# Second expert layer: 16 prompt tokens leave the dense set and gather their experts' rows instead

## The chip, the cores and the metric

The kernel runs on one core of a Trainium2 chip. The metric is the device time of one execution in microseconds (us), as the median of several runs. The engines are TensorE (PE, with its weight loads as PEld), VectorE (DVE), ScalarE (ACT), GpSimd (POOL) and SyncE (SP, which issues most DMAs).

## The reference, cut to what matters

The kernel is one inference step of a trunk with two layers over 304 tokens (T): 16 meta tokens, 256 prompt tokens and 32 sample tokens. Each layer is a mixer followed by an expert layer, and only the expert layer is touched here. It picks, per head, the 16 best of 128 x 128 single-neuron experts:

```python
s1 = einsum('thd,hkd->thk', q[..., :128], keys[:, 0])     # 8 heads, 128 keys
s2 = einsum('thd,hkd->thk', q[..., 128:], keys[:, 1])
v1, i1 = top_k(s1, 16); v2, i2 = top_k(s2, 16)
sc, pos = top_k(v1[..., :, None] + v2[..., None, :], 16)  # best 16 of 256
eidx = i1 * 128 + i2 at pos                               # one of 16384 experts
gate = softmax(sc)
act  = gelu(einsum('thkd,td->thk', u_tab[eidx], x))
y    = einsum('thk,thkd->td', gate * act, v_tab[eidx])    # rows of 1024
```

u_tab and v_tab hold 16384 rows of 1024 floats, 64 MB each.

## The kernel before, in words

`peer(l)` is the expert layer, called for layer 0 and layer 1. It treats most tokens as dense: for 256 of them every expert is evaluated, and a matrix G of gate values (zero where an expert isn't chosen) weighs the results. The other `ng` tokens are gathered: their chosen rows are fetched one by one. In layer 0, 48 tokens are gathered, as two groups of 16 and 32 tokens; in layer 1, whose meta tokens need no expert output (`d0` = 16), it is one group of 32.

Dense part. The 16384 experts are 128 blocks of 128. For a block `e`, `up_load` loads 128 rows of u (512 KB, tile `raw`), `up` multiplies them with the dense tokens into one PSUM tile `ps_u`, and a Gelu on ACT stores `act`. The first 24 blocks (nf) use full fp32 operands, of which each matmul shows as two records; the other 104 split each operand in a high and a low part (`wh` by ACT, `wl` by DVE) and take three matmuls for each of the 8 slices of the model dimension, 24 in all. `weigh` (L1029) multiplies `act` by G and splits it again (`ch`, `cl`, tiles `sc` and `qs`); `down` takes two token tiles of 128 by 512 output columns by three products, 12 matmuls, added up in `ps_mm` through all blocks. The last four blocks are kept for the end, where they are multiplied transposed ("ends"). 42 `act` tiles exist, so that 36 blocks of `up` (ahead) run before the first `down`.

G. `ggroup` builds G for 8 tokens at a time with four DVE operations, 16 matmuls in f16 and two copies by ACT, and writes 16 tokens at a time to DRAM. `gates_load` (L1013) reads it back for 8 blocks at once (1 MB, tile `gb`); the tag `gb` has four buffers, used also for the staging of G and for `xr2` and `yac` of the gathered tokens.

Gathered part. `gprep` spreads the gathered tokens' expert numbers, gates and rows over 128 partitions (8 lanes for 16 tokens, 4 for 32). For each group, `rows` fetches rows of u by an indirect DMA on POOL (128 rows, 512 KB, tile `ab`), `gup` on DVE multiplies and adds up, `gact` is the Gelu; then the same for v with `gdown`, and `gsum` adds the lanes up on TensorE.

What sets the order. Every step has a due time in `at(due, step)`; steps are emitted in that order, and the language's scheduler then places the instructions of each engine by its own estimates, so that one may pass another. Each engine runs its list strictly in that order: an instruction that waits holds up all those behind it. `late` ties the gathered steps to the last marked DVE operation. The due times hang on `tg` (start of `ggroup`), `tw` (first `down`, after all `ggroup`s), and `te` (end).

Of the kernel before, what the change touches and what calls it, by code (L numbers as in the profile page):

```python
# [8 lines left out]
F32 = mybir.dt.float32  # L9
# [30 lines left out]
def _consts():  # L40
    c = {}
    eye = np.eye(P, dtype=np.float32)
    one = np.ones((P, P), np.float32)
    c["k_all"] = np.concatenate(
        [eye, one / 1024, one / 256, np.tile(np.arange(P, dtype=np.float32), (P, 1))], axis=1)
    sm = np.ones((P, T), np.float32)
    for o, _ in CHUNKS:
        sm[:, o] = 0
    gid = np.zeros(T, np.int64)
    for i, (o, n) in enumerate(CHUNKS):  # L50
        gid[o:o + n] = i
    att = np.zeros((P, 3, P), np.float32)
    for i, (o, n) in enumerate(TT):
        for s in range(n):
            for t in range(s, n):
                att[s, i, t] = gid[o + s] == gid[o + t]
    km = np.zeros((P, 11), np.float32)
    km[:, 0] = (np.arange(P) // 16) % 2 == 0
    km[:, 1] = (np.arange(P) // 16) % 2 == 1
    km[:16, 2] = 1  # L60
    for s in range(8):
        km[16 + 4 * s:20 + 4 * s, 3 + s] = 1
    c["k_diag"] = np.concatenate(
        [np.arange(P)[:, None] % n == np.arange(n)[None] for n in (32, 16)], axis=1).astype(np.float32)
    p, r = np.arange(P)[None], np.arange(P)[:, None]
    c["k_rep"] = np.stack([r == 16 + p % 32, (r == p % 16), (r == p % 32), r // 32 == p // 32, r // 16 == p // 16],
                          axis=1).astype(np.float32)
    hs = np.eye(4, dtype=np.float32)
    xm = ((r // 32 == np.arange(64)[None] // 16) & (r % 32 < 16)).astype(np.float32)
    c["k_gla"] = np.concatenate([sm, att.reshape(P, -1), km, np.tile(hs.reshape(1, 16) / 128, (P, 1)), xm], axis=1)  # L70
    c["k_hsel"] = np.ascontiguousarray(np.repeat(hs[:, :, None], P, 2))
    rs = np.ones((P, T), np.float32)
    rs[:, 0:TP:64] = 0
    rs[:, TP::4] = 0
    q = np.arange(P)
    bo = (q[:, None] // 64 == q[None] // 64).astype(np.float32)
    r = np.arange(64)
    grp = np.where(r < 16, 0, np.where(r < 48, 1 + (r - 16) // 4, 9))
    ma = np.zeros((2, P, 2, 64), np.float32)
    for j in range(2):  # L80
        same = np.ones((64, 64), bool) if j == 0 else (grp[:, None] == grp[None]) & (grp[:, None] < 9)
        for o in range(2):
            ma[j, 64 * o:64 * o + 64, 0] = same & (r[:, None] < r[None])
            ma[j, 64 * o:64 * o + 64, 1] = same & (r[:, None] <= r[None])
    lv = np.stack([((q[:, None] // (2 * m) == q[None] // (2 * m)) & ((q[:, None] // m) % 2 == 1)
                    & ((q[None] // m) % 2 == 0)) | (q[:, None] == q[None]) for m in (1, 2, 4, 8, 16, 32)], axis=1)
    cm = np.tile(grp[None] == 0, (P, 1))
    rm = np.tile((grp[:, None] == np.arange(9)[None]), (2, 1))
    c["k_rwkv"] = np.concatenate(
        [rs, bo / 64, bo, cm, rm, bo[:, ::64] / 64], axis=1).astype(np.float32)  # L90
    c["k_inv"] = np.concatenate(
        [ma[0].reshape(P, P), ma[1].reshape(P, P), lv[:, 0].T, lv[:, 1:5].reshape(P, 4 * P)], axis=1).astype(np.float32)
    return c
# [88 lines left out]
class Prog:  # L182
# [564 lines left out]
    def peer(self, xh, xl, l):  # L747
# [1 line left out]

        nc, a = self.nc, self.a  # L750
        d0 = 0 if l == 0 else NM
        g0 = d0 + 256
        ng = T - g0
        tiles = [(d0, P), (d0 + P, P), (g0, ng)]
        groups = ([(0, 16)] if ng == 48 else []) + [(ng - 32, 32)]
        with ExitStack() as es:
            pp = es.enter_context(self.tc.tile_pool(name=f"pe{l}", bufs=1, reuse_waits="tile"))
            self.psum_banks(mm=4, u=2, s=2)
# [2 lines left out]
            pr = es.enter_context(self.tc.tile_pool(name=f"pr{l}", bufs=1, side="right", reuse_waits="tile"))  # L761
            ab = lambda shape, dt=F32: self.t(pr, shape, dt, "ab", 3)
            gb = lambda shape, dt=F32: self.t(pr, shape, dt, "gb", 4)
            G = self.t(dp, [16, P, P, 16], F32, "G")
            self.extra(pp, 3, 1)
            es.callback(self.extra, None, 0, 0)
            units = []
# [15 lines left out]


            keys = gb([P, 16, P])
            kr = tl([P, 5, P], "k_rep")
            krep, kblk = kr[:, :3, :], kr[:, 3:, :]

            vals2 = tl([P, 16, 2, 16], "vals"), tl([P, 8, 2, 16], "valsg")
            idx2 = tl([P, 16, 2, 16], "idx", 1, U32), tl([P, 8, 2, 16], "idxg", 1, U32)  # L790
# [7 lines left out]
            def whole32():  # L798
                x32.extend(tl([P, 4, 256], n) for n in ("wh", "wl"))
                self.turn.update(wh=-1, wl=-1)  # L800
                for k in range(KB):
                    nc.vector.tensor_tensor(x32[k // 4][:, k % 4, :], f(xh[:, k, d0:d0 + 256]),
                                            f(xl[:, k, d0:d0 + 256]), op=ALU.add)

            qst, pq0 = {}, []

# [183 lines left out]

            def up(e):
                wh, wl = wts.pop(("u", e))
                pu = self.psum("u")[:, :256]
                if wl is None:
                    for k in range(KB):
                        mm(nc, pu, wh[:, k, :], x32[k // 4][:, k % 4, :], k == 0, k == KB - 1)
                else:
                    mm3(nc, pu, lambda k: wh[:, k, :], lambda k: wl[:, k, :],
                        lambda k: xh[:, k, d0:d0 + 256], lambda k: xl[:, k, d0:d0 + 256])
                acts[e] = tl([P, 256], "act", NR)  # L1000
                nc.scalar.activation(acts[e], pu, AF.Gelu_apprx_tanh)  # L1001

            Y, ends = [], []
# [5 lines left out]
                                         None, hl if hl is None else (hl[:, 0], hl[:, 1]))  # L1009

            def gates_load(e):
                gr.append(gb([P, 16, 8, 16]))
                nc.sync.dma_start(gr[-1].rearrange("p b i t -> p b (i t)"),  # L1013
                                  G[:, :, e:e + 8, :].rearrange("b p i t -> p b (i t)"))

            def weigh(e):

                if e % 8 == 0:
                    gr[0] = gr.pop(1)
                if e >= P - NL:  # L1020
                    ch, cl = (tl([P, 256], "act", NR, F32R) for _ in range(2))
                elif e % 2:
                    cc = tl([P, 2, 256], "qs", 3, F32R)
                    ch, cl = cc[:, 0, :], cc[:, 1, :]
                else:
                    ch, cl = (tl([P, 256], "sc", 6, F32R) for _ in range(2))
                c = acts.pop(e)
                v16 = lambda ap: ap.rearrange("p (b t) -> p b t", t=16)
                self.mark[True] = nc.vector.tensor_tensor(v16(c), v16(c), gr[0][:, :, e % 8, :], op=ALU.mult)  # L1029
                split(nc, c, ch, cl)  # L1030
                coef[e] = ch, cl

            def down(e):
# [8 lines left out]
                for i in range(2):  # L1042
                    for j, (c, v) in enumerate(((ch, vh), (ch, vl), (cl, vh))):
                        for q in range(2):
                            mm(nc, Y[2 * q + i], c[:, i * P:(i + 1) * P],
                               v[:, 4 * q:4 * q + 4, :].rearrange("p k d -> p (k d)"),
                               e == 0 and j == 0, e == P - NL - 1 and j == 2)

# [9 lines left out]
            def gprep():  # L1058
# [11 lines left out]
                for g, (r0, n) in enumerate(groups):  # L1070
                    er, gt, eg = tl([P, n], f"er{g}", 1, I32), tl([P, n], f"gt{g}"), tl([P, n], "gres", 2)
                    o = 0 if n == 32 else 1
                    rep = krep[:ng, 2 * l + o, :]
                    for src, dst in ((ei, eg), (gates[2], gt)):
                        pt = self.psum("s")
                        mm(nc, pt[:, :P], rep, src[:ng])
# [77 lines left out]
            tg = ps + pp_["pl"]  # L1154
            for i in range(2):
                at(tg + 0.1 * i, turn, i)
            for q in range(32):
                at(tg + 1 + pp_["gs"] * q, ggroup, q)
            tw = tg + 1 + 32 * pp_["gs"] + pp_["gl"]

            for j, step in enumerate(pairs(1)):
                at(tg + 1.1 + pp_["gs"] * (8 + 1.5 * j), step)
            at(tg + 1.1 + pp_["gs"] * 31, gprep)
            ahead, u0, u1 = pp_["ahead"], pp_["u0"], pp_["us1"]
            n0 = int((tg - u0) / u1)
            for e in range(P):
# [15 lines left out]
            t1 = tw + pp_["g2"]  # L1182
            te = tw + 2 * tu * (P - ahead) + tu * ahead
            tg = (te - pp_["te"] - 15 - t1) / (2 * len(gc))
            for j, (g, c) in enumerate(gc):
                for s, fn, tab in ((0, gup, "u"), (len(gc), gdown, "v")):
                    late(t1 + tg * (j + s), rows, tab, g, c)
                    for r in range(2):
                        late(t1 + tg * (j + s + pp_["gj"] * r) + self.lag, fn, g, c, r)
            for g in range(len(groups)):  # L1190
                late(t1 + tg * len(gc) + self.lag - 0.5, gact, g)
            late(te - pp_["te"], gsum)
            for q in range(2):
                late(te - pp_["te"], xsum, q)
# [19 lines left out]
            for k in range(KB):  # L1214
                if k % 2 == 0:
                    YT[k // 2] = self.psum("u" if k < 4 else "mm")
                o = YT[k // 2][:, (k % 2) * 256:(k % 2) * 256 + 256]
                for j, args in enumerate(ends):
                    into(o, k, *args, j == 0 and k % 2 == 0, False)
                for i in range(2):  # L1220
                    mm(nc, o[:, i * P:(i + 1) * P], Ys[:, 2 * (k // 4) + i, (k % 4) * P:(k % 4 + 1) * P], self.ident,
                       False, i == 1)
                xk = X[k // 4][:, k % 4, :]
                nc.vector.scalar_tensor_tensor(z(k)[:, d0:g0], xk[:, d0:g0], ALPHA, o, op0=ALU.mult, op1=ALU.add)
# [585 lines left out]
```

## Time and profile before

| | us |
|---|---|
| median of 3 runs | 2565.35 (2559.76 to 2567.32) |
| the profiled execution, its own time | 2568.89 |
| its span, first to last instruction | 2567.1 |
| PE busy in it | 2420.2 (94%) |
| layer 1: first fp32 `up` | 1707.6 |
| layer 1: G built | 1778 to 1896 |
| layer 1: first `down` | 1918.17 |
| layer 1: last `down` | 2528 |

A time in the rows below is the start in us from the span's first instruction; matmuls overlap, so the time that one takes on PE is read from the distance between two starts, not from its duration.

### The profile page before, as it was taken

The numbers are of one execution on the slowest core, as the hardware profiler recorded it, in microseconds if no ns is written. First come the engines' busy times: TensorE is split into PE (matmuls) and PEld (weight loads), VectorE is DVE, ScalarE is ACT, GpSimd is POOL, SyncE is SP. The second block draws the span as 40 slices with busy tenths as digits, with TensorE's granted clock in tenths as the row PEclk, the third lists the DMA queues.
The fourth block names the chain that finished last, engine by engine and source line by source line (L and its number), as shares of the span: only waits on it lengthen the run. The fifth ranks groups of instructions, "written<-read, shape, count | busy, mean of one in ns | idle before, by whom it ended". The sixth has DMA issues, their size and how long they took to land.

```text
span 2567.1 us, 41284 instructions
## 1 busy us (share of the span) xinstructions
PE 2420.2 (94%) x15394; PEld 2073.1 (81%) x15402; DVE 1854.4 (72%) x4200; ACT 1155.6 (45%) x2054; POOL 550.5 (21%) x620
## 2 busy tenths in 40 slices
PE   7989989899999999988999988899989999999997
PEld 5878879799998898865666656787979999989986
DVE  5555898777767888766777785679767766677775
ACT  7524335444444445523544443432444444444453
POOL 3435100011111222024334233520010101121200
PEclk9978999999999999989999999899999999999998
DMA  5323246897879978622111102323679767797662
GB/s 160 114 73 124 99 153 229 283 308 284 285 272 304 364 274 286 240 94 85 48 50 46 40 29 91 119 89 140 233 261 314 245 245 254 261 338 263 242 220 72
DMA packets 197873, 489.73 MB, mean 191 GB/s; under 512 B 21396, under 2 KB 91428, under 8 KB 192936
## 3 DMA queue, kind: packets, MB, share of 16 engines
q1 hardware_dynamic: 173480, 401.10, 44.6%
q0 software_dynamic: 23040, 83.90, 9.7%
q8 instruction: 121, 1.98, 0.3%
q10 hardware_dynamic: 1152, 2.10, 0.2%
q14 instruction: 80, 0.66, 0.1%
HBM read 447.41 MB, written 39.63 MB: 190 GB/s over the span
## 4 chain that ended last, share of the span: by engine, by line
PE 75%; DVE 13%; issue 3%; DMA 3%; ACT 3%; POOL 2%; SPq 1%; POOLq 0%; ACTq 0%; DVEq 0%
PE ps_mm L162 33%; PE ps_u L162 24%; PE ps_s L162 7%; PE ps_pj L162 4%; PE ps_iv L162 3%; DMA gb<-G 3%; PE ps_ch L162 1%; DVE wl L171 1%; PE ps_po L162 1%; DVE ab L921 1%; ACT wh L170 0%; DVE ab L923 0%; DVE x L1575 0%; DVE x L375 0%; DVE ab L918 0%
## 5 line engine op out<-in xcount | busy, mean ns | idle before, releaser
L170 ACT ACTIVATE wh<-raw 128x1024 fp32r<-128x1024 f32 x529 | 560.3, 1060 | 634.4 <-PE ps_u L162 302.1
L171 DVE TENSOR_TENSOR wl<-raw,wh 128x1024 fp32r<-128x1024 f32 x481 | 594.2, 1236 | 301.9 <-ACT wh L170 295.9
L162 PE MATMUL ps_u<-xh,wl 128*128 128x256 f32 x1664 | 469.8, 282 | 5.5 <-DVE wl L171 5.5
L162 PE MATMUL ps_u<-xh,wh 128*128 128x256 f32 x1664 | 471.8, 284 | 2.6 <-ACT act L1001 2.6
L162 PE MATMUL ps_u<-xl,wh 128*128 128x256 f32 x1664 | 468.2, 281 | 0.0
L162 PEld LDWEIGHTS ps_u<-xh,wh 128*128 128x128 f32 x1664 | 314.7, 189 | 11.4 <-ACT act L1001 3.0
L162 PEld LDWEIGHTS ps_u<-xl,wh 128*128 128x128 f32 x1664 | 314.4, 189 | 8.9 <-issue 0.8
L162 PEld LDWEIGHTS ps_u<-xh,wl 128*128 128x128 f32 x1664 | 314.3, 189 | 6.9 <-DVE wl L171 6.6
L162 PE MATMUL ps_mm<-wh,sc 128*128 128x512 f32 x992 | 292.0, 396 | 12.3 <-ACT sc L170 12.3
L162 PE MATMUL ps_mm<-wh,qs 128*128 128x512 f32 x992 | 291.8, 396 | 0.0
L1092 POOL DMA_INDIRECT ab<-in_u,er x80 | 76.8, 961 | 862.9 <-DVE ab L1099 478.7
L162 PEld LDWEIGHTS ps_mm<-wh,sc 128*128 128x128 f32 x992 | 181.8, 190 | 46.6 <-ACT sc L170 12.7
L162 PEld LDWEIGHTS ps_mm<-wh,qs 128*128 128x128 f32 x992 | 181.5, 189 | 35.0
L1092 POOL DMA_INDIRECT ab<-in_v,er x80 | 103.8, 1298 | 431.6 <-DVE gb L1113 339.2
L162 PE MATMUL ps_mm<-wl,sc 128*128 128x512 f32 x496 | 155.4, 395 | 0.1
L162 PE MATMUL ps_mm<-wl,qs 128*128 128x512 f32 x496 | 155.2, 394 | 0.0
L1001 ACT ACTIVATE act<-ps_u 128x256 f32<-128x256 f32 x256 | 94.1, 368 | 105.8 <-PE ps_u L162 105.8
L162 PE MATMUL ps_mm<-xh,wh 128*128 128x304 f32 x416 | 134.0, 326 | 8.1 <-ACT xh L353 4.2
L162 PE MATMUL ps_s<-ab 128*128 128x128 f16 x1024 | 133.6, 296 | 1.7 <-ACT gb L970 1.3
L162 PE MATMUL ps_mm<-xh,wl 128*128 128x304 f32 x416 | 130.1, 313 | 3.9 <-POOL wl L171 3.3
L171 POOL TENSOR_TENSOR wl<-raw,wh 128x1024 fp32r<-128x1024 f32 x48 | 115.2, 2405 | 79.9 <-ACT wh L170 72.5
L162 PE MATMUL ps_mm<-xl,wh 128*128 128x304 f32 x416 | 130.4, 314 | 1.8 <-POOL xl L358 1.8
(559 smaller groups left out, 4492.2 us busy)
## 6 DMA issues: line engine op xcount, KB each, us to landing
raw<-in_ut SPq DMA_DIRECT2D x256, 512.0 KB
raw<-in_v SPq DMA_DIRECT2D x256, 512.0 KB
G<-gb SPq DMA_DIRECT2D x32, 1024.0 KB
gb<-G SPq DMA_DIRECT2D x32, 1024.0 KB
raw<-in_wq SPq DMA_DIRECT2D x32, 512.0 KB
raw<-in_w_in SPq DMA_DIRECT2D x20, 512.0 KB
raw<-in_w_out SPq DMA_DIRECT2D x8, 512.0 KB
raw<-in_w_k SPq DMA_DIRECT2D x8, 512.0 KB
```

The lines of the kernel that those rows point to most:

```text
L162: nc.tensor.matmul(out, lhsT, rhs, start=start, stop=stop, skip_group_check=True)
L170: nc.scalar.activation(h, src, AF.Copy)
L171: return (eng or nc.vector).tensor_tensor(l, src, f(h), op=ALU.subtract)
L921: nc.vector.tensor_tensor(eqj, eqj, ib[:n, :, None, :].to_broadcast([n, 16, 16, nh]), op=ALU.mult)
L1001: nc.scalar.activation(acts[e], pu, AF.Gelu_apprx_tanh)
L1092: nc.gpsimd.indirect_dma_start(out=w[:, j, :], out_offset=None, in_=a[f"{tab}{l}"], in_offset=bass.IndirectOffsetOnAxis(ap=gst[g][0][:, c ...
```

## The change

Layer 1 takes 240 dense tokens instead of 256 (`ND = (256, 240)`). The 16 prompt tokens that leave join the 32 sample tokens: 48 are gathered, in the two groups that layer 0 has. The dense tokens still make two tiles of 128, which now start at 0 and at 112 and overlap by 16 tokens. `up`, its Gelu, the weighing and the splits run over 240 columns; `down` keeps its matmuls as they are (the 16 tokens of the overlap are computed twice, and one of the two is left out at the end). G has 15 pieces instead of 16, so 30 `ggroup` steps instead of 32, and every due time behind them moves up by two such steps, 5.7 units. There are 32 more gathers of 128 rows, 16 for u and 16 for v, with 16 more `gup` and 16 more `gdown`. The delay `lag` between a gather and its use is now a minimum of three terms: 20 becomes 19.29 in both layers.

```diff
+ND = (256,240)
...
-        g0 = d0 + 256
+        nd = ND[l]
+        g0 = d0 + nd
         ng = T - g0
-        tiles = [(d0, P), (d0 + P, P), (g0, ng)]
-        groups = ([(0, 16)] if ng == 48 else []) + [(ng - 32, 32)]
+        toff = (0, nd - P)
+        tiles = [(d0 + o, P) for o in toff] + [(g0, ng)]
+        groups = [(0, ng - 32)] * (ng > 32) + [(ng - 32, 32)]
...
-                c = slice(i * P, (i + 1) * P)
+                c = slice(toff[i], toff[i] + P)
...
-                pu = self.psum("u")[:, :256]
+                pu = self.psum("u")[:, :nd]
...
-                            mm(nc, Y[2 * q + i], c[:, i * P:(i + 1) * P],
+                            mm(nc, Y[2 * q + i], c[:, toff[i]:toff[i] + P],
...
-            for q in range(32):
+            for q in range(nd // 8):
                 at(tg + 1 + pp_["gs"] * q, ggroup, q)
-            tw = tg + 1 + 32 * pp_["gs"] + pp_["gl"]
+            tw = tg + 1 + (nd // 8) * pp_["gs"] + pp_["gl"]
...
-            at(tg + 1.1 + pp_["gs"] * 31, gprep)
+            at(tg + 1.1 + pp_["gs"] * max(nd // 8 - 1, 27.75), gprep)
...
+            lag = min(self.lag, 2.4 * tg, 14 + tg / 2)
...
-                        late(t1 + tg * (j + s + pp_["gj"] * r) + self.lag, fn, g, c, r)
+                        late(t1 + tg * (j + s + pp_["gj"] * r) + lag, fn, g, c, r)
...
-                    mm(nc, o[:, i * P:(i + 1) * P], Ys[:, 2 * (k // 4) + i, (k % 4) * P:(k % 4 + 1) * P], self.ident,
+                    mm(nc, o[:, i * P:nd if i else P], Ys[:, 2 * (k // 4) + i, (k % 4) * P:(k % 4 + 1) * P], self.ident[:, i * (2 * P - nd):],
```

Beyond these counts the scheduler's lists come out differently at three places of layer 1; layer 0's lists move by a few DVE rows.

SP, at the first loads of gates (`gb<-G`) behind the last pieces of G. Before:

```order
501 L972 DMA G_15998<-gb_18671 128x2048
502 L249 DMA raw_18979<-in_ut 128x1024
503 L249 DMA raw_19017<-in_v 128x1024
504 L1013 DMA gb_18901<-G_15998 128x16x128
505 L249 DMA raw_19035<-in_ut 128x1024
506 L249 DMA raw_19075<-in_v 128x1024
507 L249 DMA raw_19093<-in_ut 128x1024
508 L1013 DMA gb_19260<-G_15998 128x16x128
509 L249 DMA raw_19131<-in_v 128x1024
```

The same place of the changed kernel:

```order
499 L252 DMA raw_18930<-in_v 128x1024
500 L252 DMA raw_18948<-in_ut 128x1024
501 L979 DMA G_15998<-gb_18619 128x2048
502 L1020 DMA gb_18870<-G_15998 128x15x128
503 L1020 DMA gb_19214<-G_15998 128x15x128
504 L1020 DMA gb_19698<-G_15998 128x15x128
505 L1020 DMA gb_20163<-G_15998 128x15x128
506 L252 DMA raw_18986<-in_v 128x1024
507 L1020 DMA gb_20629<-G_15998 128x15x128
508 L1020 DMA gb_21092<-G_15998 128x15x128
509 L1020 DMA gb_21558<-G_15998 128x15x128
510 L252 DMA raw_19004<-in_ut 128x1024
```

Two or three loads of weights stood between two loads of gates; now seven loads of gates have one load of weights among them, and the next weights (`raw_19004`) stand behind all seven.

DVE, from the first weighing (L1029, L1036 in the changed kernel) on; `wl` is the low part of a block of weights, which an `up` or a `down` needs. Before:

```order
2586 L1029 TENSOR_TENSOR act_16949<-act_16949,gb_18901 128x256
2587 L1029 TENSOR_TENSOR act_16984<-act_16984,gb_18901 128x256
2588 L1029 TENSOR_TENSOR act_17047<-act_17047,gb_18901 128x256
2589 L171 TENSOR_TENSOR sc_18904<-act_16949,sc_18903 128x256
2590 L1029 TENSOR_TENSOR act_17080<-act_17080,gb_18901 128x256
2591 L1029 TENSOR_TENSOR act_17259<-act_17259,gb_18901 128x256
2592 L171 TENSOR_TENSOR wl_19020<-raw_19017,wh_19019 128x1024
2593 L171 TENSOR_TENSOR qs_18957<-act_16984,qs_18957 128x256
```

In the changed kernel the first weighing is row 2579. Rows 2579 to 2618 are 33 weighings (the last of them reads the fifth load, `gb_20629`), six splits of weighed tiles and one `wl`; then:

```order
2614 L1036 TENSOR_TENSOR act_18341<-act_18341,gb_20163 128x240
2615 L1036 TENSOR_TENSOR act_18426<-act_18426,gb_20163 128x240
2616 L1036 TENSOR_TENSOR act_18514<-act_18514,gb_20163 128x240
2617 L1036 TENSOR_TENSOR act_18608<-act_18608,gb_20163 128x240
2618 L1036 TENSOR_TENSOR act_18763<-act_18763,gb_20629 128x240
2619 L174 TENSOR_TENSOR wl_18840<-raw_18837,wh_18839 128x1024
2620 L1036 TENSOR_TENSOR act_18796<-act_18796,gb_20629 128x240
2621 L174 TENSOR_TENSOR wl_18896<-raw_18893,wh_18895 128x1024
```

`wl_18840` belongs to the `up` that PE has in its list right before the first `down` (`ps_u_18843`). Before, two to eight weighings stood between two `wl`.

ACT, at the first splits of weighed tiles (`sc` and `qs`). Before, the Gelus (`act<-ps_u`, L1001) of the last blocks of `up` stood ahead of the first of them:

```order
1507 L1001 ACTIVATE act_18827<-ps_u_18802 128x256
1508 L170 ACTIVATE wh_18926<-raw_18924 128x1024
1509 L1001 ACTIVATE act_18860<-ps_u_18835 128x256
1510 L170 ACTIVATE wh_18981<-raw_18979 128x1024
1511 L1001 ACTIVATE act_18899<-ps_u_18874 128x256
1512 L170 ACTIVATE sc_18903<-act_16949 128x256
```

The same place of the changed kernel, where L1008 is the Gelu:

```order
1502 L173 ACTIVATE sc_18872<-act_16949 128x240
1503 L173 ACTIVATE qs_18926<-act_16984 128x240
1504 L173 ACTIVATE sc_18981<-act_17047 128x240
1505 L173 ACTIVATE qs_19040<-act_17080 128x240
1506 L173 ACTIVATE sc_19095<-act_17259 128x240
1507 L173 ACTIVATE qs_19154<-act_17272 128x240
1508 L173 ACTIVATE wh_18833<-raw_18831 128x1024
1509 L1008 ACTIVATE act_18763<-ps_u_18738 128x240
1510 L173 ACTIVATE wh_18839<-raw_18837 128x1024
```

Six splits, which need weighed tiles, now stand ahead of the Gelu of `ps_u_18738`. `ps_u` has two banks, so the second `up` after that one has to wait for this Gelu. PE's own list has 96 matmuls of `up` between the last matmul of G and the first `down` before; now it has 46 up to that wait, 24 behind it (`ps_u_18804`), and 24 more (`ps_u_18843`) that need `wl_18840`.

DVE, at the second run of weighings, behind `gact` (`ha<-ha,gt`), where the buffers of `xr2` come free. In the changed kernel four loads of gates are weighed here (32 weighings) in rows 2871 to 2902; between them stand `wl_22189` (row 2878) and `wl_22207` (row 2885), and then:

```order
2899 L1036 TENSOR_TENSOR act_21938<-act_21938,gb_23890 128x240
2900 L1036 TENSOR_TENSOR act_21997<-act_21997,gb_23890 128x240
2901 L1036 TENSOR_TENSOR act_22056<-act_22056,gb_23890 128x240
2902 L1036 TENSOR_TENSOR act_22115<-act_22115,gb_23890 128x240
2903 L174 TENSOR_TENSOR wl_22246<-raw_22243,wh_22245 128x1024
```

Before, the first 32 of these weighings have nine `wl` among them (rows 2860 to 2906).

## Rows read from the trace of the kernel before

**Rows 1.** The page: busy time of each engine, share of the span, instructions.

```profile
PE 2420.2 (94%) x15394; PEld 2073.1 (81%) x15402; DVE 1854.4 (72%) x4200; ACT 1155.6 (45%) x2054; POOL 550.5 (21%) x620
```

**Rows 2.** Busy time by stretches, clock as a share of 2.4 GHz.

```profile
core 0: us, PE busy (x) PEld busy (x) DVE busy (x) ACT busy (x) POOL busy (x), PEclk, DMA share, GB/s
600.00:664.00 64.00, 64.00 (x415) 58.36 (x414) 49.04 (x66) 30.92 (x47) 9.36 (x10) 1.00 0.79 284
1749.00:1753.00 4.00, 4.00 (x11) 3.23 (x12) 4.00 (x23) 0.17 (x1) 0.00 (x0) 0.57 0.02 4
1778.00:1896.00 118.00, 115.85 (x858) 108.78 (x857) 100.48 (x180) 56.31 (x95) 0.00 (x0) 0.99 0.59 217
1918.00:1922.00 4.00, 3.83 (x9) 3.06 (x10) 4.00 (x11) 2.56 (x7) 0.00 (x0) 0.50 1.12 339
2048.00:2112.00 64.00, 64.00 (x408) 57.95 (x407) 42.40 (x54) 31.21 (x48) 7.50 (x8) 1.00 0.72 253
```

**Rows 3.** Timeline of PE, one `up` of layer 1: start, duration, instruction.

```profile
2049.95 0.28 PE L162 MATMUL ps_u<-xh,wh 128*128 128x256 f32 x1
...
2052.80 0.63 PE L162 MATMUL ps_mm<-wh,sc 128*128 128x512 f32 x2
```

**Rows 4.** Timeline of PE, matmuls of other widths.

```profile
180.41 0.30 PE L162 MATMUL ps_mm<-yl,wh 128*128 128x304 f32 x1
180.55 0.30 PE L162 MATMUL ps_mm<-yh,wl 128*128 128x304 f32 x1
...
1710.43 1.89 PE L162 MATMUL ps_u<-wl,raw 128*128 128x256 f32 x8
...
1781.37 2.04 PE L162 MATMUL ps_s<-ab 128*128 128x128 f16 x16
...
2534.20 0.60 PE L162 MATMUL ps_u<-k_all,ab 128*128 128x128 f32 x4
2534.64 0.39 PE L162 MATMUL ps_mm<-k_all,ab 128*128 128x128 f32 x2
```

**Rows 5.** The lines of `gsum` on PE: durations, first and last start.

```profile
L162 PE MATMUL ps_s<-k_diag,gb x16: 193/276/276, 2512.2 to 2513.8; 128*128 128x32 f32 x16
```

**Rows 6.** Timeline of PE around the first `down`, idle time in brackets.

```profile
1748.95 1.55 PE L162 MATMUL ps_u<-wh,raw 128*128 128x256 f32 x4 [4.52 <-ACT act L1001]
...
1895.72 0.77 PE L162 MATMUL ps_s<-ab 128*128 128x128 f16 x5
...
1899.48 1.88 PE L162 MATMUL ps_s<-ab,k_rep 32*128 32x512 f32 x4
...
1911.49 0.28 PE L162 MATMUL ps_u<-xl,wh 128*128 128x256 f32 x1
1918.17 1.22 PE L162 MATMUL ps_mm<-wh,sc 128*128 128x512 f32 x2 [6.40 <-ACT sc L170]
```

**Rows 7.** Timeline of SP's queue, from the first load of gates on.

```profile
1902.03 0.38 SPq L1013 DMA_DIRECT2D gb<-G  x1
...
1934.78 0.43 SPq L1013 DMA_DIRECT2D gb<-G  x1
...
2232.80 0.43 SPq L1013 DMA_DIRECT2D gb<-G  x1
```

**Rows 8.** Timeline of DVE: weighings (L1029) and splits.

```profile
1917.24 1.10 DVE L1029 TENSOR_TENSOR act<-act,gb 128x256 f32<-128x256 f32 x3 [5.27 <-DMA gb<-G]
1918.25 0.42 DVE L171 TENSOR_TENSOR sc<-act,sc 128x256 fp32r<-128x256 f32 x1
...
1943.40 0.76 DVE L1029 TENSOR_TENSOR act<-act,gb 128x256 f32<-128x256 f32 x2 [0.67 <-DMA gb<-G]
...
2240.18 0.76 DVE L1029 TENSOR_TENSOR act<-act,gb 128x256 f32<-128x256 f32 x2 [2.16 <-DMA gb<-G]
```

**Rows 9.** Timeline of PE: its idle time at the second run of weighings.

```profile
2277.30 0.39 PE L162 MATMUL ps_u<-xh,wl 128*128 128x256 f32 x1 [1.41 <-DVE wl L171]
```

**Rows 10.** DVE by lines, 1896 to 2530: busy, mean ns, idle before.

```profile
L171 DVE TENSOR_TENSOR wl<-raw,wh 128x1024 fp32r<-128x1024 f32 x220 | 270.2, 1229 | 156.6 <-ACT wh L170 155.5
```

More of the change, by code (lines that the diff above doesn't have):

```diff
@@ L65, in _consts @@
     p, r = np.arange(P)[None], np.arange(P)[:, None]
-    c["k_rep"] = np.stack([r == 16 + p % 32, (r == p % 16), (r == p % 32), r // 32 == p // 32, r // 16 == p // 16],
+    c["k_rep"] = np.stack([r == 16 + p % 32, (r == p % 16), (r == p % 32), r == 32 + p % 32,
+                             r // 32 == p // 32, r // 16 == p // 16],
                           axis=1).astype(np.float32)
@@ L751, in peer @@
         d0 = 0 if l == 0 else NM
-        g0 = d0 + 256
+        nd = ND[l]
+        g0 = d0 + nd
         ng = T - g0
-        tiles = [(d0, P), (d0 + P, P), (g0, ng)]
-        groups = ([(0, 16)] if ng == 48 else []) + [(ng - 32, 32)]
+        toff = (0, nd - P)
+        tiles = [(d0 + o, P) for o in toff] + [(g0, ng)]
+        groups = [(0, ng - 32)] * (ng > 32) + [(ng - 32, 32)]
+        reps = {(0, 16): 1, (0, 32): 2, (16, 32): 0, (32, 32): 3}
         with ExitStack() as es:
@@ L763, in peer @@
             gb = lambda shape, dt=F32: self.t(pr, shape, dt, "gb", 4)
-            G = self.t(dp, [16, P, P, 16], F32, "G")
+            G = self.t(dp, [nd // 16, P, P, 16], F32, "G")
             self.extra(pp, 3, 1)
@@ L785, in peer @@
             keys = gb([P, 16, P])
-            kr = tl([P, 5, P], "k_rep")
-            krep, kblk = kr[:, :3, :], kr[:, 3:, :]
+            kr = tl([P, 6, P], "k_rep")
+            krep, kblk = kr[:, :4, :], kr[:, 4:, :]
             vals2 = tl([P, 16, 2, 16], "vals"), tl([P, 8, 2, 16], "valsg")
@@ L801, in whole32 @@
                 for k in range(KB):
-                    nc.vector.tensor_tensor(x32[k // 4][:, k % 4, :], f(xh[:, k, d0:d0 + 256]),
-                                            f(xl[:, k, d0:d0 + 256]), op=ALU.add)
+                    nc.vector.tensor_tensor(x32[k // 4][:, k % 4, :nd], f(xh[:, k, d0:d0 + nd]),
+                                            f(xl[:, k, d0:d0 + nd]), op=ALU.add)
             qst, pq0 = {}, []
@@ L992, in up @@
                 wh, wl = wts.pop(("u", e))
-                pu = self.psum("u")[:, :256]
+                pu = self.psum("u")[:, :nd]
                 if wl is None:
                     for k in range(KB):
-                        mm(nc, pu, wh[:, k, :], x32[k // 4][:, k % 4, :], k == 0, k == KB - 1)
+                        mm(nc, pu, wh[:, k, :], x32[k // 4][:, k % 4, :nd], k == 0, k == KB - 1)
                 else:
                     mm3(nc, pu, lambda k: wh[:, k, :], lambda k: wl[:, k, :],
-                        lambda k: xh[:, k, d0:d0 + 256], lambda k: xl[:, k, d0:d0 + 256])
-                acts[e] = tl([P, 256], "act", NR)
+                        lambda k: xh[:, k, d0:d0 + nd], lambda k: xl[:, k, d0:d0 + nd])
+                acts[e] = tl([P, 256], "act", NR)[:, :nd]
                 nc.scalar.activation(acts[e], pu, AF.Gelu_apprx_tanh)
@@ L1011, in gates_load @@
             def gates_load(e):
-                gr.append(gb([P, 16, 8, 16]))
+                gr.append(gb([P, 16, 8, 16])[:, :nd // 16])
                 nc.sync.dma_start(gr[-1].rearrange("p b i t -> p b (i t)"),
@@ L1020, in weigh @@
                 if e >= P - NL:
-                    ch, cl = (tl([P, 256], "act", NR, F32R) for _ in range(2))
+                    ch, cl = (tl([P, 256], "act", NR, F32R)[:, :nd] for _ in range(2))
                 elif e % 2:
                     cc = tl([P, 2, 256], "qs", 3, F32R)
-                    ch, cl = cc[:, 0, :], cc[:, 1, :]
+                    ch, cl = cc[:, 0, :nd], cc[:, 1, :nd]
                 else:
-                    ch, cl = (tl([P, 256], "sc", 6, F32R) for _ in range(2))
+                    ch, cl = (tl([P, 256], "sc", 6, F32R)[:, :nd] for _ in range(2))
                 c = acts.pop(e)
@@ L1072, in gprep @@
                     o = 0 if n == 32 else 1
-                    rep = krep[:ng, 2 * l + o, :]
+                    rep = krep[:ng, reps[r0, n], :]
                     for src, dst in ((ei, eg), (gates[2], gt)):
@@ L1188, in peer @@
                     for r in range(2):
-                        late(t1 + tg * (j + s + pp_["gj"] * r) + self.lag, fn, g, c, r)
+                        late(t1 + tg * (j + s + pp_["gj"] * r) + lag, fn, g, c, r)
             for g in range(len(groups)):
-                late(t1 + tg * len(gc) + self.lag - 0.5, gact, g)
+                late(t1 + tg * len(gc) + lag - 0.5, gact, g)
             late(te - pp_["te"], gsum)
@@ L1216, in peer @@
                     YT[k // 2] = self.psum("u" if k < 4 else "mm")
-                o = YT[k // 2][:, (k % 2) * 256:(k % 2) * 256 + 256]
+                o = YT[k // 2][:, (k % 2) * 256:(k % 2) * 256 + nd]
                 for j, args in enumerate(ends):
```

## The prediction

> **What bounds the kernel now.** I read the page first: PE is busy 94% of the span, DVE 72%, and the other engines less [rows 1]. An average says little, so the stretches come next. Deep in layer 1's expert stage PE is busy for all 64.00 us of a 64 us stretch, at full clock (2.4 GHz), with DVE at 42.40 us and the DMA engines at 0.72 [rows 2]. There every nanosecond of a matmul counts, and nothing else does. Then I looked for the places where PE isn't full: while G is built (115.85 of 118 us, with DVE at 100.48 [rows 2]); right before the first `down`, where PE is idle for 6.40 us until a weighed tile comes [rows 6]; and one wait of 1.41 us for a `wl` in the second run of weighings [rows 9]. The first of these two has a cause that the rows show: DVE waits for the first load of gates, issued at 1902.03 and weighed from 1917.24 on, 15.2 us later [rows 7, 8], while PE has run out of `up` work at 1911.6 [rows 6]. So two things decide: how much shorter the matmuls get, and whether PE goes on being fed at those places.
>
> **What gets shorter.** The profiled execution took 2568.89 us, 3.5 more than the median; I make the sum as a difference and apply it to the median, 2565.35.
>
> *Split `up`.* 24 matmuls take from 2049.95 to 2052.80 [rows 3], 118.8 ns each at 256 columns. At 304 columns the distance is 140 ns [rows 4], so a column costs about 0.44 ns and 240 columns would take 111.8 ns, unless a floor comes first. What the floor is the trace doesn't show at this shape. The nearest rows have 128 columns: 110 ns from 2534.20 to 2534.64 (four), and 118 ns in the f16 products of G (16 in 2.04 us, less about 0.27 for the last one's own length) [rows 4]. Gain per matmul between 0.8 and 7.0; I take 6.5, since the row at 110 ns has the same unstrided weights and the f16 row reads its weights with a stride. 104 blocks x 24 = 2496 matmuls: **-16** (0 to -17.5). The Trainium skill (TensorE: Matmul & The Clock Gate, section on LDWEIGHTS) says that a weight load costs by its columns, about columns / 1.2 ns; for 128 that is an estimate of 107 ns, which speaks against any gain below some 107 ns; the row at 110 agrees, the f16 row at 118 does not, and by the first the gain stays near -16, by the second it falls to -2.
>
> *fp32 `up`.* Eight records end 1.89 us after the first starts; with 0.3 to 0.4 for the last one's own length they start 213 to 227 ns apart [rows 4], I take 216; at 240 of 256 columns that is 202. 24 blocks x 16 records x 13.5 ns: **-5** (0 to -5.5).
>
> *G.* Two `ggroup` steps fewer are 32 matmuls of 118 ns: **-4**. But G's stretch has DVE at 85% and PE idle for only 2.15 us [rows 2]; the `up`s in it shrink by some 3 us while DVE's work per step stays, so PE waits for DVE instead. I give back **+3.5** (0 to +7).
>
> *Ends.* 96 matmuls of 256 columns: **-0.5**. Sum of the gains: -25.5, and -22 after G.
>
> **What is added.** `gprep`'s second group costs PE some 2.3 us (1.88 for four records of 512 columns [rows 6], and the small ones); it falls into the wait before the first `down` and is counted there. `gsum`'s second group is 16 more records: 16 from 2512.2 to 2513.8, 0.107 each [rows 5]: **+1.7**, with nothing beside it. 32 more gathers, 16 `gup` and 16 `gdown` go to POOL, the DMA queues and DVE. Layer 0 gathers 48 tokens already: there, PE is busy 64.00 of 64 us with DVE at 49.04 and DMA at 0.79 [rows 2]. So in steady state they are hidden: 0 (to +6, if layer 1 gets less room).
>
> **What the new order costs.** Two places, both on the chain to the end since PE makes up for nothing later.
>
> *First `down`.* Before, PE has 96 `up` matmuls after G's last one and works until 1911.6, 15.4 us [rows 6]. Now it reaches the wait for a PSUM bank after 46: 15.4 - 96 x 0.119 + 46 x 0.112 + 2.3 = 11.5 us. That bank is freed by a Gelu which ACT has behind six splits of weighed tiles. The first weighing came 21.0 us after G's last matmul (1896.2 to 1917.24 [rows 6, 8]); six weighings and five splits at 0.335 (three from 1917.24 to 1918.25 [rows 8]) are 3.7, and a weight split on ACT, priced like DVE's 1.23 [rows 10], makes it about 4.9 more until the Gelu. If the gates land as late as before, PE waits 21.0 + 4.9 - 11.5 = 14.4 us; if 4 us sooner, since no weight loads are queued ahead of the second load, 10.4. I take 12.4. Then come 24 matmuls (2.7 us), and the next `up` needs `wl_18840`, behind 33 weighings of which the last needs the fifth load of gates. Three `gb` buffers are free at that point, so the fourth load waits for the first eight weighings (about 5 us after the first) and the fifth for the next eight (about 9). From issue to first weighing a load takes 8.6 us (1934.78 to 1943.40) or 7.4 (2232.80 to 2240.18) [rows 7, 8]: the fifth can be weighed 17 us after the first, and `wl` takes 1.23 [rows 10]. PE is through with its 24 matmuls about 7.6 us after the first weighing, so it waits 18.4 - 7.6 = 10.8 us more. Together 23 against 6.4: **+16.8**. Ends: +4 (if the loads land in a row and DVE is through its 33 weighings in 11 us) and +26 (if only two buffers are free).
>
> *Second run of weighings.* Between `wl_22144`, the last one ahead of `gact`, and `wl_22246` DVE has 32 weighings, fed by four loads, and only two `wl`. The fourth load can start once the first has been weighed: 7.4 for the first, 4.1 for its eight weighings and a `wl`, 8.5 for the fourth, 3 for its weighings and the `wl`: 23 us. PE uses a `wl` each 2.8 us (24 `up` in 2.85 [rows 3]), so three of them last 8.4 us, and DVE is at most two ahead (5.6): PE waits between 9 and 14.6 us; I take 11.9, against 1.4 now [rows 9]: **+10.5** (0, if the loads come early enough, to +13).
>
> *Clock.* After the idle time of 6.40 us PE's clock is at 0.50 (1.2 GHz) for a whole stretch of 4 us, and after one of 4.52 at 0.57 [rows 6, 2]. Each such stretch of 4 us costs about half of its length. One exists now; the new waits make three or four: **+4** (0 to +8).
>
> Sum: -25.5 + 3.5 + 1.7 + 16.8 + 10.5 + 4 = **+11**. Forecast: 2565.35 + 11 = 2576 us (2580 in a profiled execution); with every term within half of its bounds, 2564 to 2590.
>
> **The rivals.**
> *PE stays fed* (faster). The lists only look bad: seven loads of gates run back to back and land early, weighings at 0.335 us go past quickly, and the weights behind them arrive in time. The waits then stay near those of before, and -22 + 1.7 plus about 2 for each place gives -16: 2549. For it: steady stretches have DVE at 66% [rows 2], room to catch up. Against it: the `wl` that PE needs stands behind a fifth load that can't start before DVE has weighed sixteen blocks. It decides if the two places together cost less than about 12 us. Chance 0.17.
> *The up matmuls keep their 119 ns* (slower still). If the floor is that of the f16 row, 14 of the -16 are lost: 2590. For it: a weight load goes with each matmul, and 128 columns of f16 take 118 [rows 4]. Against it: 110 in the other row. Chance 0.13.
> *The loads take longer.* Six gathers, three loads of gates and two of weights now start together while the DMA engines already show 1.12 of their share [rows 2]; at 15 us per load in place of 8, the first `down` costs another 14 and the second run 7: 2597. Chance 0.1.
> *In between* (no change): only one of the two places waits, -16 + 13 = -3 or so: 2563. Chance 0.12.
> That leaves 0.48 for the forecast.
>
> **How the numbers follow.** Within 0.3% is 7.7 us, about what a measurement of this kernel can tell from no change. Faster by more: the first rival, 0.17. Slower by more: both slower rivals, and of the forecast the part above 2573, some 0.42: 0.65. The rest is 0.18. The range reaches to the rival that is faster, and on the other side to 2603, so that each end leaves out about one in ten.
>
> **What would show it.** Right: start distances of 111 to 113 ns in layer 1's `up`; idle time of PE of some 12 us ended by ACT and some 10 ended by DVE `wl` before the first `down`; several waits for `wl` in the second run, 10 to 14 us in all; clock 0.5 after each. Wrong: distances near 119; waits before the first `down` under 10 us together; or PE idle in the steady stretch with POOL's gathers or the DMA share near 1, which would mean that the added gathers aren't hidden.

## The result, and the profile after

The changed kernel takes 2586.31 us (median of 11 runs) against 2567.32 before (11 runs): ratio 1.0077, 95% interval 1.0054 to 1.0099, some 19 us slower. Forecast was 2576 in a range of 2549 to 2603, slower by 11. Its profiled span is 2587.0 us, against 2567.1 before; the two spans differ by 1.2 us where layer 1's expert stage starts, so the rest is all in that stage.

The page, busy time of each engine (answers to [rows 1]):

```profile
PE 2422.8 (94%) x15394; PEld 2075.3 (80%) x15394; DVE 1879.9 (73%) x4246; ACT 1151.7 (45%) x2053; POOL 621.1 (24%) x652
```

PE's busy time hardly moved, which hides both sides: shorter matmuls, and others drawn out by a halved clock (PEclk 0.50 in the rows below). The stretches show more (columns as in [rows 2]):

```profile
1775.00:1889.00 114.00, 107.83 (x809) 102.92 (x808) 100.41 (x210) 54.14 (x90) 0.00 (x0) 0.96 0.60 213
1903.00:1915.00 12.00, 0.29 (x3) 0.10 (x2) 4.73 (x15) 3.42 (x9) 0.00 (x0) 0.67 1.14 325
1915.00:1920.00 5.00, 5.00 (x24) 5.00 (x25) 5.00 (x14) 1.07 (x2) 0.00 (x0) 0.50 0.87 234
1920.00:1927.00 7.00, 0.82 (x4) 0.54 (x3) 4.87 (x14) 1.32 (x2) 0.00 (x0) 0.74 1.17 312
2048.00:2112.00 64.00, 64.00 (x422) 57.74 (x421) 47.97 (x66) 31.89 (x49) 13.53 (x12) 1.00 0.83 284
2245.00:2253.00 8.00, 0.29 (x2) 0.00 (x0) 3.25 (x8) 1.06 (x2) 0.00 (x0) 0.72 1.13 285
```

In steady state (2048 to 2112) PE is full as before and does 422 matmuls where it did 408: the added gathers hide, and the shorter `up` pays. Twice before the first `down`, and again at 2245, PE does next to nothing. What it waits for, from 1836 to 2547 (us in total, times, longest):

```profile
PE ps_u L165 <- ACT act L1008: 11.7, 1, 11.7
PE ps_mm L165 <- DVE wl L174: 10.2, 2, 8.0
PE ps_u L165 <- DVE wl L174: 6.6, 1, 6.6
PE ps_s L165 <- DVE ge L914: 3.2, 1, 3.2
PE ps_s L165 <- DVE ab L969: 2.9, 2, 2.6
```

The chain that leads there is read on SP and DVE. SP's timeline after G (answers to [rows 7]):

```profile
1897.31 17.89 SPq L1020 DMA_DIRECT2D gb<-G  x4
1916.62 0.34 SPq L252 DMA_DIRECT2D raw<-in_v  x1
1918.53 6.66 SPq L1020 DMA_DIRECT2D gb<-G  x3
1927.38 1.40 SPq L252 DMA_DIRECT2D raw<-in_ut  x1
```

DVE's timeline (answers to [rows 8]):

```profile
1910.27 1.04 DVE L1036 TENSOR_TENSOR act<-act,gb 128x240 f32<-128x240 f32 x3 [14.47 <-DMA gb<-G]
...
1915.38 1.21 DVE L174 TENSOR_TENSOR wl<-raw,wh 128x1024 fp32r<-128x1024 f32 x1
1916.51 7.19 DVE L1036 TENSOR_TENSOR act<-act,gb 128x240 f32<-128x240 f32 x22
1925.82 0.41 DVE L1036 TENSOR_TENSOR act<-act,gb 128x240 f32<-128x240 f32 x1 [2.11 <-DMA gb<-G]
1926.14 1.22 DVE L174 TENSOR_TENSOR wl<-raw,wh 128x1024 fp32r<-128x1024 f32 x1
```

DVE again, at the second run of weighings:

```profile
2249.76 2.32 DVE L1036 TENSOR_TENSOR act<-act,gb 128x240 f32<-128x240 f32 x7 [9.55 <-DMA gb<-G]
...
2257.37 5.18 DVE L1036 TENSOR_TENSOR act<-act,gb 128x240 f32<-128x240 f32 x16
2262.47 1.21 DVE L174 TENSOR_TENSOR wl<-raw,wh 128x1024 fp32r<-128x1024 f32 x1
```

And PE's (answers to [rows 6, 9]):

```profile
1914.92 0.57 PE L165 MATMUL ps_u<-xh,wh 128*128 128x240 f32 x1 [11.71 <-ACT act L1008]
...
1927.41 0.57 PE L165 MATMUL ps_u<-xh,wl 128*128 128x240 f32 x1 [6.59 <-DVE wl L174]
...
2253.26 1.22 PE L165 MATMUL ps_mm<-wl,qs 128*128 128x512 f32 x2 [7.98 <-DVE wl L174]
...
2263.74 0.73 PE L165 MATMUL ps_mm<-wl,sc 128*128 128x512 f32 x2 [2.24 <-DVE wl L174]
```

Up to 1927.4 these rows are one chain. The first load of gates is weighed 13 us after its issue; six weighed tiles are split before ACT gets to the Gelu at which PE stands; 22 weighings in a row, and one that waits for the fifth load, stand ahead of the `wl` that ends PE's second wait at 1927.4. The fifth load went out at 1918.5, when DVE had weighed sixteen blocks. The second run repeats it: a late load, then 16 weighings ahead of the `wl` that PE waits for.

### The profile page after: what moved, and what is told of

The parts are those of the page before. It is cut to its first block, busy times and chain, and to the rows that moved or that the text cites. A ratio compares the mean times of both kernels' runs of the same rounds, so it can differ in the third digit from the quotient of the medians.

```text
span 2587.0 us, 41407 instructions
## 1 busy us (share of the span) xinstructions
PE 2422.8 (94%) x15394; PEld 2075.3 (80%) x15394; DVE 1879.9 (73%) x4246; ACT 1151.7 (45%) x2053; POOL 621.1 (24%) x652
## 3 DMA queue, kind: packets, MB, share of 16 engines
q0 software_dynamic: 27648, 100.68, 11.5%
## 5 line engine op out<-in xcount | busy, mean ns | idle before, releaser
L165 PE MATMUL ps_u<-xh,wh 128*128 128x256 f32 (+1 forms) x1664 | 470.0, 282 | 13.0 <-ACT act L1008 13.0
L165 PE MATMUL ps_u<-xh,wl 128*128 128x256 f32 (+1 forms) x1664 | 468.2, 281 | 7.6 <-DVE wl L174 7.3
L165 PE MATMUL ps_u<-xl,wh 128*128 128x256 f32 (+1 forms) x1664 | 467.8, 281 | 0.0
L165 PEld LDWEIGHTS ps_u<-xh,wl 128*128 128x128 f32 x1664 | 319.5, 192 | 8.9 <-DVE wl L174 8.6
L1099 POOL DMA_INDIRECT ab<-in_u,er x96 | 103.9, 1083 | 867.8 <-DVE ab L1106 489.2
L1099 POOL DMA_INDIRECT ab<-in_v,er x96 | 145.3, 1513 | 385.6 <-DVE gb L1120 320.5
L1008 ACT ACTIVATE act<-ps_u 128x256 f32<-128x256 f32 (+1 forms) x256 | 92.5, 362 | 100.4 <-PE ps_u L165 100.3
```

The source lines that it names most:

```text
L165: nc.tensor.matmul(out, lhsT, rhs, start=start, stop=stop, skip_group_check=True)
L1099: nc.gpsimd.indirect_dma_start(out=w[:, j, :], out_offset=None, in_=a[f"{tab}{l}"], in_offset=bass.IndirectOffsetOnAxis(ap=gst[g][0][:, c ...
```

## The experiments

Theory A: the loss lies in the lists, which place weighings and loads of gates ahead of the weights that PE needs. Rivals: the added load of gathers and second group (B), a part of each (C), and for single runs those named there (D, E). All ratios are to the kernel before, from runs on the same chip, with their 95% intervals; times against the changed kernel are differences of such ratios. The diffs are shortened to the lines that matter.

**1. Bound the weighings.** Each weighing of layer 1 is queued behind the weight split of the `down` four blocks earlier.

```diff
 def weigh(e):
+    with ExitStack() as q:
+        if l == 1 and e - 4 in wlm:      # wlm[e]: DVE's split of v, block e
+            q.enter_context(self.tc.issue_after(wlm[e - 4]))
+        weigh_now(e)                     # the old body
```

> The changed kernel, where a weighing of layer 1 may stand at most four blocks ahead of the weight split of its own block's v in DVE's list (issue order only; nothing else is edited). Theory A, the loss lies in the lists (weighings and loads of gates placed far ahead of the weights that PE needs): the 6.6 us before the first down that end with wl and the 7.98 and 2.24 us of the second run go, with the half clock behind them; the 11.7 us that end with the Gelu stay. About 20 us less than the changed kernel, ratio to before 0.997 to 1.002. Theory B, the loss is load (32 more gathers, a second group): the waits stay or move, ratio 1.006 to 1.01. Theory C, a mixture: ratio 1.003 to 1.006.

Ratio 0.9972 (0.9955 to 0.9989), 27 us less than the changed kernel. PE's waits, 1836 to 2515:

```profile
PE ps_u L165 <- ACT act L1008: 11.2, 1, 11.2
PE ps_s L165 <- DVE ab L969: 2.9, 2, 2.6
PE ps_u L165 <- DVE wl L174: 0.8, 1, 0.8
```

The waits for `wl` are gone but for 0.8 us, and the wait for the Gelu stays, as theory A said.

**2. Most of the added gathers left out.**

```diff
-gc = [(g, c) for g in range(len(groups)) for c in range(0, groups[g][1], 2)]
+gc = [(g, c) for g in range(len(groups)) for c in range(0, groups[g][1] if g or l == 0 else 2, 2)]
...                                      # gact: the same two columns
```

> The changed kernel without 28 of its 32 added gathers and their gup and gdown (the first group of layer 1 fetches 2 of its 16 columns; the experts' rows of its 16 tokens are otherwise left out). The lists keep the seven loads of gates and the 33 weighings in a row. Theory A: no change against the changed kernel within 4 us, ratio to before 1.006 to 1.01, the same waits of about 12, 7 and 10 us. Theory B: most of the 19 us goes, ratio 0.995 to 1.002.

Ratio 1.0078 (1.0055 to 1.0101): no change that can be told, with the same waits:

```profile
PE ps_u L165 <- ACT act L1008: 11.6, 1, 11.6
PE ps_mm L165 <- DVE wl L174: 8.9, 2, 6.1
PE ps_u L165 <- DVE wl L174: 6.4, 1, 6.4
```

The gathers' number costs nothing that can be measured. With it falls theory B as far as the gathers go; the second group's `gprep` and `gsum` are still in this run.

**3. Wide matmuls back, all else changed.**

```diff
-pu = self.psum("u")[:, :nd]
+pu = self.psum("u")[:, :256]             # xh, xl and x32 to d0 + 256 as well
```

> The changed kernel, whose up matmuls in layer 1 run over 256 columns again (the last 16 columns are left unused; G, gathers, weighing and all else as in the change). By the sum of matmuls alone it should be slower than the changed kernel by some 21 us (2496 x 6.3 ns + 384 x 13 ns), ratio to before 1.015 or more: theories B and C. Theory A says more: the lists come out as before with these wider matmuls (two or three loads of weights between loads of gates), so the waits of 6.6 and 10 us go and the first one shrinks to about 4; the 21 us that the matmuls cost and the 25 to 30 us that the waits and the clock give back make it faster than the changed kernel by 4 to 10, ratio to before 1.003 to 1.006.

Ratio 1.0016 (0.9994 to 1.0037): 16 us *faster* than the changed kernel (I expected 4 to 10), although its matmuls take some 21 us more, by the estimate above. The second group is still there, so theory B falls with this run. SP's list has weights between the loads of gates again:

```profile
1892.22 0.38 SPq L1020 DMA_DIRECT2D gb<-G  x1
1898.88 0.33 SPq L252 DMA_DIRECT2D raw<-in_v  x1
1899.25 0.43 SPq L1020 DMA_DIRECT2D gb<-G  x1
1901.95 7.01 SPq L252 DMA_DIRECT2D raw<-in_ut  x1
```

Its longest waits:

```profile
PE ps_mm L165 <- ACT sc L173: 4.1, 1, 4.1
PE ps_u L165 <- DVE wl L174: 1.4, 2, 0.8
```

**4. Narrow matmuls alone, in the kernel before.**

```diff
-pu = self.psum("u")[:, :256]
+pu = self.psum("u")[:, :256 if l == 0 else 240]      # moving operands cut likewise
...
+nc.scalar.activation(acts[e][:, nd:], pu[:, :16], AF.Copy)      # layer 1 alone
```

> The kernel before, whose up matmuls in layer 1 run over 240 columns only (the last 16 columns of act are a copy of the first 16, by one small ACT operation per block; no second group, no other edit). By the matmuls alone 21 us faster than before, ratio 0.992: theories B and C with the matmuls at 112 ns. Theory A: the shorter matmuls by themselves turn the lists (weighings and loads of gates far ahead), so it is slower than before by 8 to 18 us, ratio 1.003 to 1.007, with waits of about 13 and 6 to 10 us before the first down and 10 in the second run.

The last 16 columns of `act` are filled by a copy, so this run leaves out the true experts' outputs of 16 tokens. Ratio 1.004 (1.0024 to 1.0055): slower by 10 us, with fewer columns to compute and no second group. Its SP list has three loads of gates in a row, one load of weights, and three more:

```profile
1900.92 13.80 SPq L1015 DMA_DIRECT2D gb<-G  x3
1918.21 0.34 SPq L249 DMA_DIRECT2D raw<-in_ut  x1
1920.55 7.83 SPq L1015 DMA_DIRECT2D gb<-G  x3
```

PE's waits:

```profile
PE ps_u L162 <- ACT act L1003: 14.3, 1, 14.3
PE ps_mm L162 <- DVE wl L171: 10.7, 3, 5.5
PE ps_s L162 <- ACT gb L970: 4.9, 1, 4.9
PE ps_u L162 <- DVE wl L171: 4.3, 3, 3.8
```

Runs 3 and 4 together show that the width of `up` turns the lists: with all else of the change but wide matmuls they don't turn, and with narrow matmuls and no second group they do. Run 4 alone couldn't tell the width from its small copy on ACT in each block; the copy by itself wasn't run.

**5. The same bound in the kernel before.** The edit of run 1.

> The kernel before with the same bound of four blocks on the weighings of layer 1 as in the first experiment. Theory A (the bound helps the changed kernel because it undoes lists that the change turned): here it finds little to undo, only the wait of 1.41 us in the second run; ratio to before 0.998 to 1.000. Theory D, that the bound is a gain of its own, unconnected with the change: ratio 0.990 to 0.994, as much as between the changed kernel and the first experiment.

Ratio 1.0001 (0.9978 to 1.0024). The bound is no gain of its own; theory D, that it is one, falls.

**6. A bound of sixteen blocks**, else as run 1.

> The changed kernel with a bound of sixteen blocks. If the number of weighings ahead of the weights sets the waits (theory A), about half of them comes back: before the first down 12 us and then 3, in the second run 6 instead of 10; ratio to before 1.000 to 1.004, between the first experiment (0.997) and the changed kernel (1.008). If it is only where the first few stand, the same as with four.

Ratio 1.0025 (1.0003 to 1.0047), between run 1 and the changed kernel, and the wait in the second run is 7.3 us. The 3 us expected before the first `down` didn't show.

**7. Bound of two, gathers held.** The bound in both layers, and POOL copies one element of the first weighed tile, behind which the gathers are queued. It asks whether the gathers lengthen the first loads of gates (theory E).

```diff
+if e == 0:
+    gp[0] = nc.gpsimd.tensor_copy(tiny, f(coef[0][0][:1, :1]))
...
+with self.tc.issue_after(gp[0]):
     nc.gpsimd.indirect_dma_start(...)
```

> The changed kernel with a bound of two blocks in both layers, and the gathers of each layer held on POOL behind the first weighed tile (one element copied by POOL, in whose list the gathers stand behind it). What is open is what the wait of 11 to 12 us before the first down is made of. If the six gathers of 512 KB that start with the first loads of gates lengthen those loads (theory E), the first weighing comes 4 to 6 us sooner, the wait shrinks to 4 to 6 us in layer 1 and by as much in layer 0; ratio to before 0.988 to 0.993. If the load of gates takes its 13 us by itself, the wait stays at 9 to 10 us; ratio 0.994 to 0.997.

Ratio 0.9901 (0.9879 to 0.9924), 2540.35 us, the lowest median of all, though run 9's interval overlaps. Some 19 us of its gain lie ahead of layer 1's expert stage, which starts at 1689.8 in place of 1708.8, since both edits act in layer 0 too. Its waits from 1836 to 2494:

```profile
PE ps_s L165 <- DVE ab L969: 2.9, 2, 2.6
PE ps_u L165 <- ACT act L1008: 2.8, 1, 2.8
```

```profile
1884.33 0.73 DVE L1047 TENSOR_TENSOR act<-act,gb 128x240 f32<-128x240 f32 x2 [7.81 <-DMA gb<-G]
```

This first weighing comes 14.7 us after G's last matmul (1869.67); in the changed kernel it was 21.4 (1888.9 to 1910.27). In the kernel before it is 21.0, and 14.6 with the same edits (run 9). The bound alone leaves it at 21.5 (run 1), the hold alone brings 15.0 (run 10). So the six gathers that start with the first loads had put off the first weighing by some 6 to 7 us in both kernels.

**8. The rest of the diff.** `ND = (256, 256)` in the changed kernel.

> The changed kernel with 256 dense tokens in both layers again: what is left of the diff is the delay lag of 19.29 instead of 20 and the constant with one more matrix. All theories: no difference, ratio to before 0.998 to 1.002.

Ratio 0.9996 (0.9977 to 1.0014): no difference that can be told.

**9. The edits of run 7 in the kernel before.**

> The kernel before with the same two edits as the seventh experiment (bound of two blocks in both layers, gathers held behind the first weighed tile). It asks what the change is worth once the lists and the gathers' start are the same. If the matmuls' 25 us are realised there, it is slower than the seventh experiment by some 10 or more after gprep, gsum and the stage of G have taken their 8 to 12: ratio to before 0.993 to 0.997. If the change gives nothing even then: 0.989 to 0.991, the same as the seventh.

Ratio 0.991 (0.9889 to 0.9932): a miss; I expected 0.993 to 0.997. With the same bound and the same start of the gathers the change is worth 2 us and not 10, with some 8 us of uncertainty by the two intervals, so that it can't be told from nothing. Where its gain goes is counted below.

**10. Gathers held, no bound.**

> The changed kernel with the gathers of each layer held behind the first weighed tile, without a bound on the weighings. Theory E alone would give 10 us back over both layers. But the 33 weighings still stand ahead of wl in layer 1, so what the first wait gives back the second takes: first down after about 7 us and then up to 16; layer 0 gains about 5; the second run stays at 10. Ratio to before 1.002 to 1.008.

Ratio 1.0056 (1.0034 to 1.0079). The first wait shrinks and the second grows, since the weighings still stand ahead of `wl`:

```profile
PE ps_u L165 <- DVE wl L174: 13.8, 1, 13.8
PE ps_mm L165 <- DVE wl L174: 10.5, 2, 7.6
PE ps_u L165 <- ACT act L1008: 5.4, 1, 5.4
```

**11. Run 4 with the bound of run 1.**

> The kernel of the fourth experiment (before, with up over 240 columns only, the last 16 columns of act a copy of the first) with the bound of four blocks on the weighings of layer 1. If the turned lists are the whole reason why the shorter matmuls alone made it slower, the waits for wl before the first down and in the second run go, and only a wait of 12 to 14 us for a Gelu is left; ratio to before 0.994 to 0.998. If the shorter matmuls lose their 21 us elsewhere: 1.000 or more.

Ratio 0.9978 (0.996 to 0.9996), 16 us less than run 4; the waits for `wl` are gone but for 0.3 us, and one of 14.1 us for the Gelu is left, with one of 4.9 for ACT within G that run 4 has too. So it was the lists that made the kernel with narrow matmuls slower.

## Why the prediction was right, and where its sizes were off

By stretches of layer 1's expert stage in the two profiled spans, before and after: to the start of G's matmuls 70.6 and 66.5; G 118.0 and 113.7; from there to the first `down` 22.0 and 42.8; to the last `down` 609.5 and 614.3; the tail 39.4 and 41.0. Sum of the differences: -4.1 - 4.3 + 20.8 + 4.8 + 1.6 = +18.8.

*Split `up`*: right. The distance is 112.4 ns, from 2049.78 to 2052.48 for 24:

```profile
2049.78 0.27 PE L165 MATMUL ps_u<-xh,wh 128*128 128x240 f32 x1
...
2052.48 0.63 PE L165 MATMUL ps_mm<-wh,sc 128*128 128x512 f32 x2
```

2496 x 6.4 ns = 16.0, forecast 16; the rival with matmuls kept at 119 ns falls, and with it the f16 row's 118 ns as a floor for this shape. But 240 columns are close to a floor: in `gsum` records of 32 columns, and of 16 in the changed kernel, start 112 ns apart at full clock too (the 0.107 of [rows 5] takes in a first distance of 28 ns). A still narrower `up` would probably win little; no run tried one. The Trainium skill's rule (TensorE: Matmul & The Clock Gate, section on LDWEIGHTS) gives an estimate of 107 ns for these weights; the measured 112 lies a little above it. *fp32 `up`*: 203 ns per record, forecast 202.

*G*: as forecast, the stretch gives back most of its gain: DVE is at 100.41 us of 114, PE's idle time rises from 2.2 to 6.2 us. Of the 4.3 us by which the stretch is shorter, 2.7 are 24 `up` matmuls that now stand behind it.

*First `down`*: the mechanism as forecast, at its places: 11.7 us ended by ACT (forecast 12.4), then 6.6 by `wl` (forecast 10.8). That the first of them came out so near is luck: the gates came no sooner than before, 21.4 us after G's last matmul and not 19, and PE had work for 14.3 us and not 11.5. The second is shorter since the fifth load was weighed 15.5 us after the first and not 17, and since the 26 matmuls before it took 5.9 us and not the 2.7 of 24. Idle time was 5 us less than forecast; the clock made up for it.

*Second run*: 10.2 us in two waits, forecast 11.9. The first load was issued at 2239.44 and weighed from 2249.76, with DVE idle for 9.55 us.

*Clock*: the step that was undersized. I took +4, with whole stretches of 4 us per wait. The granted clock was at half (1.2 GHz) for 13.7 us after the first wait began and 6.8 after the second, 10.2 in the second run, and also before and within G and at `gsum`: 58 us in all in the stage ahead of the tail, against 14 before. PE was busy in 40 of them and in 12 of those before; as matmuls take about twice as long there (in `gsum` they start 214 ns apart in place of 112), this is an estimate of +14 in place of +4. The 26 matmuls between the two waits alone took 5.9 us (1914.92 to 1920.82, where the second wait began) in place of 2.9. Adding up each matmul's time above its usual one, the second run cost 13.3 us against 2.3 before, that is 2 more than its added idle time.

*`gsum`*: forecast +1.7, measured +5. Its 32 records take 4.2 us, from 2525.63 to 2529.84, against 1.7 for 16 before, and the clock is at half from 2528.4 for 6.8 us (part of the 58), which draws out the `down` matmuls behind by 2.5. The trace of before had a sign of it: behind the 32 records of layer 0's `gsum` the clock is 0.51 from 1094 to 1100.

```profile
2525.63 4.39 PE L165 MATMUL ps_s<-k_diag,gb 128*128 128x16 f32 x32
```

*Left out*: `down`, whose matmuls I took as unchanged, is slower by 23 ns per block, some 3 us (see the last section).

*Rivals*: "PE stays fed" fell at its condition: the two places cost about 30 us and not under 12. "In between" and longer loads fell as well; the fifth load wasn't at 15 us from issue but at 7.3 (1918.5 to 1925.8). Only the first one was near it, with 13.0, and it had taken 15.2 before.

So the mechanism was right, and its sizes partly cancel. Against the forecast of +11 there are some 5 us less of idle time in all, 9 more for the clock (the tail has 1.5 less of it than before), and 5 more of work: 3 in `down`, and 2.5 in `gprep`'s second group, which the forecast took off the wait before the first `down` and added nowhere. That makes +20, where +19 was measured.

What I hadn't seen in the prediction is how the cause hangs together: I listed the turned lists beside the 16 gathered tokens, as two costs of one change. Runs 3 and 4 show that the narrower `up` turns them, gathers or not; run 9 shows that even without that the change would be worth some 2 us. There, from run 9 to run 7, the stage before G gains 4.3 us and G 4.2; up to the first `down` 8.6 are lost (the second group of `gprep`, a wait of 2.8, 7.8 us at half clock); between first and last `down`, 5.7 are won of the 14.0 that the matmuls save: 2.9 go to 26 `up` matmuls more that stand there, 2.8 to the slower `down` below, and 2.6 are left for `gsum` and 3.4 us at half clock; the tail loses 1.2. That last split is worked out from rows, not shown by a run of its own.

## What to carry to other kernels

Where a scheduler orders the queues by its own estimates, a shorter instruction can reorder work that has nothing to do with it; compare the lists and find, for each engine that feeds the bottleneck, the first instruction that it now has to wait for. Work that is ready early but needed late (here the weighings) wants a bound on how far it may run ahead, since each item in a strict queue that waits for a load holds up those that don't. And a wait can cost more than its length: here the 26 matmuls behind the wait of 11.7 us ran at half clock and took 3 us more.

## What the runs showed of the hardware that I hadn't expected

The twelve matmuls of a `down`, 512 columns each, take 2794.5 ns in the changed kernel and 2771.5 before (means of 48 blocks in steady state). Leaving out the gathers doesn't change it (run 2: 2794.7); with the same overlapping tiles but 256-column `up` it is 2782.5 (run 3), and with 240-column `up` but tiles at 0 and 128 it is 2767.8 (run 4). So the second tile's start at column 112 in place of 128 goes with 11 ns more at the wide `up` and 27 at the narrow one, some 2 ns per matmul and 3 us in all. It isn't the place of the tiles alone, since the width of `up` changes it by 12 ns with the same tiles; why, stays open.

In the changed kernel the clock fell to half at 1750.1 and 1770.6, behind idle times of 2.72 and 2.51 us, yet 2.90 us of idle time in layer 0 of the kernel before left it at full:

```profile
856.54 0.39 PE L162 MATMUL ps_u<-xh,wl 128*128 128x256 f32 x1 [2.90 <-DVE wl L171]
```

And in `gsum` of the changed kernel it fell with no idle time at all, while behind the 32 records of layer 0's `gsum` it stayed at full in run 9 (1.00 from 1085.9 to 1096). The length of an idle time alone doesn't tell whether the clock falls.
